# Seven block products in place of eight for some pairs of up products, and four down groups in place of three

## The chip, the cores and the metric

The kernel runs on one core of a Trainium2 chip. The metric is the device time of one execution in microseconds. The kernel before takes 1869.24 us (median of 3 runs, 1866.7 to 1871.07).

## The reference, cut to what matters

One step of a small diffusion backbone with 640 tokens (128 context tokens and 512 latent tokens), width 1024 and two layers: the first mixes tokens with a gated DeltaNet, the second with neighbourhood attention. Each layer ends with a gated feed-forward part, and that is what the change touches:

```python
def conv_ffn(h, w_up, conv_w, conv_b, w_down):
    u = dwconv_centred(h @ w_up, conv_w) + conv_b
    val, gate = jnp.split(u, 2, axis=-1)
    return (jax.nn.silu(gate) * val) @ w_down
...
xs = xs + g2s * conv_ffn(rmsnorm(xs, norm2_g[l]) * (1.0 + sc2s) + sh2s, ffn_w_up[l], ...)
```

The up projection is 1024 x 5632, the down projection 2816 x 1024, all in float32. The shifts, scales and gates of a layer come from a product of 1024 x 6144 with the conditioning vector.

## The kernel before, in words

Activations lie transposed: partitions carry channels, the free axis carries the 640 tokens. A float32 factor is split into a high part, rounded to the fast matmul format fp32r (`hh`, `wh`, by ScalarE), and the remainder (`hl`, `wl`, by VectorE). A product of a 128-channel tile with a k-tile is three matmuls, high x high, high x low, low x high (`pass3`, L388 to L390), accumulated in PSUM over eight k-tiles. The tokens are cut at 384, so that a product has matmuls of 384 and of 256 columns.

A feed-forward layer (`ffn`) goes through 22 pairs of up products. A pair is a value tile (`uv`) and its gate tile (`ug`): `weights` loads 512 KB on SP's queue into one of two staging tiles (`wst`), casts and subtracts it into one of two weight buffers (`wh`, `wl`), and the product goes into a PSUM tile of two banks, of which there are two (tag `d`). `conv` (L440, L445) takes it out: one ScalarE activation for the middle tap, four VectorE steps for the outer taps of the two token groups. Then silu, the product of value and gate, and the split into `F` follow. After 8, 7 and 7 pairs the down products of that group of `F` tiles run for the eight output tiles (`rdn`), and `residual` (L454) adds them, times the gate of the modulation, into the residual stream `X` with three VectorE steps an output tile. The last group is cut into two halves of tokens (`into_residual_split`), so that the next norm begins while the second half is still multiplied.

Modulation vectors that are needed later are computed beside this by VectorE alone (`ada_rows`, L252): a row tile of 256 KB is loaded and two multiply-reduce instructions of 512 columns follow. `between` hands out those of 32 modulation tiles after the products of the first layer, and `Na.run` those of 16 more in the attention stage; eight are left to the second layer. In the feed-forward layers their loads are issued from GpSimd's queue, in the attention stage from SP's.

The order of instructions on each engine is fixed when the kernel is built: a scheduler takes for each engine the earliest instruction of the program whose inputs it expects to be ready, so work without dependencies is drawn forward into gaps. `issue_after` (through `behind`, `chained`) ties one instruction's place behind another's; `high_priority` moves a block forward. At run time every engine and queue works strictly in that order.

Of the kernel before, what the change touches and what calls it, by code (L numbers as in the profile page):

```python
# [57 lines left out]
GROUPS = ((0, 8), (8, 15), (15, 22))  # L58
# [29 lines left out]
class Net:  # L88
    def __init__(self, ctx, tc, a):
# [5 lines left out]
        self.wide = False  # L95
        self.hooks, self.strict = [], False
# [313 lines left out]
    def dense(self, src, name, base=UBASE, halves=HALVES_U):  # L410
        w = self.weights(src, KT, name)
        ps = self.pd.tile([128, 1024], F32, tag="d", name=f"d{name}")
        for cols in halves:
            self.prod(ps, base, w, KT, self.hmov, cols)
        return ps
# [4 lines left out]
    def dense_many(self, srcs, names, norm):  # L420
# [11 lines left out]
        return [ps for _, ps in out]  # L432

# [24 lines left out]

    def into_residual(self, srcs, kt, movs, l, gi, name, first={}, between=None):
        late = []  # L460
        for m in range(KT):
            w = first.get(m) or self.weights(srcs[m], kt, f"{name}{m}")
            ps = self.pd.tile([128, 1024], F32, tag="d", name=f"r{name}{m}")
            if m < 2:
                late.append((w, ps))
                for half in (0, 1):
                    self.prod(ps, RBASE, w, kt, movs, HALVES_R[half], ks=range(kt - 1))
                if m < 1:
                    continue
            else:  # L470
                late = [(w, ps)]
            for i, (w, ps) in enumerate(late, m + 1 - len(late)):
                for half in (0, 1):
                    self.prod(ps, RBASE, w, kt, movs, HALVES_R[half], ks=range(kt - 1, kt) if m < 2 else None)
                for half in (0, 1):
                    self.residual(ps, i, half, l, gi)
            if between and m > 1:
                between(None)

    def half_bank(self, name, i, half):  # L480
        if self.wide and i % 2 == 1:
            return self.pa.tile([128, 512], F32, tag="g", name=name)
        return self.pd.tile([128, 1024 if self.wide else 512], F32, tag="d", name=name)
# [41 lines left out]
    def ffn(self, l, fp, norm, norms, between=None):  # L525
# [3 lines left out]
        fcb = self.smv("fcb").rearrange("p (l t) -> p l t", l=2)[:, l]  # L529
        def hold(name, n):  # L530
            if name[-1] == "5":
                return fp.tile([128, 2 * W], F32R, tag="F", name=name, bufs=9)[:, 16 : 16 + n]
            size = KT if name[-1] in "01" else NFT - GROUPS[-1][0]
            return fp.tile([128, size * 128], F32R, tag=name[:2] + name[-1], name=name, bufs=1)[:, :n]

        for grp, (g0, g1) in enumerate(GROUPS):
            fs = []
            srcs = [a["w_dn"][l, m][:, g0 * 128 : g1 * 128] for m in range(KT)]
            first = {}
            for i in range(g0, g1):  # L540
                if i >= g1 - 2:
                    m = i - g1 + 2
                    first[m] = self.weights(srcs[m], g1 - g0, f"dn{l}{grp}{m}", None, hold)
                up, names = [a["w_up"][l, i], a["w_up"][l, NFT + i]], [f"uv{l}{i}", f"ug{l}{i}"]
                if i == 0:
                    with self.behind(self.marks):
                        pv, pg = self.dense_many(up, names, norm)
                else:
                    pv = self.dense(up[0], names[0])
                    if between:  # L550
                        between(None)
                    pg = self.dense(up[1], names[1])
                with self.tc.high_priority(FHP if i == g1 - 1 else 0):
                    yv = fp.tile([128, W], F32, tag="yv", name=f"yv{l}{i}", bufs=2)
                    yg = fp.tile([128, W], F32, tag="yg", name=f"yg{l}{i}", bufs=2)
                    self.conv(yv, pv, fcw[:, i], fcb[:, i : i + 1])
                    self.conv(yg, pg, fcw[:, NFT + i], fcb[:, NFT + i : NFT + i + 1])
                    c = slice(0, W)
                    nc.scalar.activation(yg[:, c], yg[:, c], AF.Silu)
                    nc.vector.tensor_tensor(yv[:, c], yv[:, c], yg[:, c], ALU.mult)  # L560
                    f = fp.tile([128, 2 * W], F32R, tag="F", name=f"F{l}{i}", bufs=9).rearrange("p (a w) -> p a w", a=2)
                    nc.scalar.copy(f[:, 0, c], yv[:, c])
                    nc.vector.tensor_tensor(f[:, 1, c], yv[:, c], f[:, 0, c].bitcast(F32), ALU.subtract)
                fs.append(f)
                if between:
                    between(i)
            movs = lambda k, fs=fs: (fs[k][:, 0, :], fs[k][:, 1, :])
            if g1 < NFT:
                self.into_residual(srcs, g1 - g0, movs, l, 5, f"dn{l}{grp}", first, between)
            else:  # L570
# [1094 lines left out]
```

## Time and profile before

| | us |
|---|---|
| median of 3 runs | 1869.24 |
| profiled execution | 1872.86 |
| its span, first to last instruction | 1871.1 |
| TensorE busy, of the span | 1790.4 (96%) |
| VectorE busy | 1257.4 (67%) |
| ScalarE busy | 725.9 (39%) |
| GpSimd busy | 290.3 (16%) |

The first feed-forward layer runs from about 583 to 1050 us, the attention stage to about 1350, the second feed-forward layer from about 1397 to the end. The mean granted TensorE clock is 0.98. Matmuls are pipelined: their listed durations overlap, and the ends of VectorE's instructions overlap a little with the next start. A row of a group of instructions gives engine, operation, output and inputs by the program's names, shape, count, then busy time in us and mean duration in ns, then the idle time before them and what ended it. L12 is line 12 of the kernel.

### The profile page before, as it was taken

The numbers are of one execution on the slowest core, as the hardware profiler recorded it, in microseconds if no ns is written. First come the engines' busy times: TensorE is split into PE (matmuls) and PEld (weight loads), VectorE is DVE, ScalarE is ACT, GpSimd is POOL, SyncE is SP. The second block draws the span as 40 slices with busy tenths as digits, with TensorE's granted clock in tenths as the row PEclk, the third lists the DMA queues.
The fourth block names the chain that finished last, engine by engine and source line by source line (L and its number), as shares of the span: only waits on it lengthen the run. The fifth ranks groups of instructions, "written<-read, shape, count | busy, mean of one in ns | idle before, by whom it ended". The sixth has DMA issues, their size and how long they took to land.

```text
span 1871.1 us, 34463 instructions
## 1 busy us (share of the span) xinstructions
PE 1790.4 (96%) x13587; PEld 1702.7 (91%) x13587; DVE 1257.4 (67%) x3093; ACT 725.9 (39%) x1461; POOL 290.3 (16%) x498
## 2 busy tenths in 40 slices
PE   6889999799999999999999999999999999999998
PEld 5878988598899999999999988888899999999998
DVE  6797867487678999754465799555689643543664
ACT  4553445264444341241243444444454322332343
POOL 0245103417003112100000212111141000000000
PEclk9898999799999999999999999999999999999999
DMA  7133233232242455441222344222334312222231
GB/s 299 61 85 108 54 124 108 76 96 61 64 158 86 155 182 163 132 163 54 87 90 80 124 152 139 75 78 65 96 107 136 102 48 78 88 62 77 89 92 57
DMA packets 102482, 194.17 MB, mean 104 GB/s; under 512 B 39496, under 2 KB 59034, under 8 KB 99560
## 3 DMA queue, kind: packets, MB, share of 16 engines
q1 hardware_dynamic: 93376, 161.57, 27.5%
q0 software_dynamic: 8400, 29.87, 5.2%
q8 instruction: 107, 1.75, 0.4%
q14 instruction: 55, 0.45, 0.1%
q10 hardware_dynamic: 544, 0.52, 0.1%
HBM read 183.09 MB, written 12.46 MB: 105 GB/s over the span
## 4 chain that ended last, share of the span: by engine, by line
PE 50%; DVE 4%; issue 2%; DMA 1%; ACT 1%; POOL 0%; DVEq 0%; POOLq 0%; ACTq 0%
PE duv L388 4%; PE duv L390 4%; PE duv L389 4%; PE dug L388 4%; PE dug L389 4%; PE dug L390 4%; PE rdn L388 4%; PE rdn L389 4%; PE rdn L390 4%; PE dqn L388 1%; PE dvn L388 1%; PE no L1346 1%; PE s L1289 1%; PE dvn L390 1%; PE dvn L389 1%
## 5 line engine op out<-in xcount | busy, mean ns | idle before, releaser
L388 PE MATMUL duv<-hh,whuv 128*128 128x256 f32 (+1 forms) x704 | 217.2, 309 | 5.9 <-DVE yv L445 4.0
L388 PE MATMUL rdn<-F,whdn 128*128 128x384 f32 (+1 forms) x704 | 216.1, 307 | 3.3 <-DVE X L454 3.3
L390 PE MATMUL duv<-hh,wluv 128*128 128x256 f32 (+1 forms) x704 | 216.7, 308 | 0.3 <-DVE wluv L378 0.3
L389 PE MATMUL duv<-hl,whuv 128*128 128x256 f32 (+1 forms) x704 | 216.5, 308 | 0.0
L389 PE MATMUL dug<-hl,whug 128*128 128x256 f32 (+1 forms) x704 | 215.9, 307 | 0.0
L390 PE MATMUL dug<-hh,wlug 128*128 128x256 f32 (+1 forms) x704 | 215.9, 307 | 0.0
L388 PE MATMUL dug<-hh,whug 128*128 128x256 f32 (+1 forms) x704 | 215.9, 307 | 0.0
L389 PE MATMUL rdn<-F,whdn 128*128 128x384 f32 (+1 forms) x704 | 215.5, 306 | 0.0
L390 PE MATMUL rdn<-F,wldn 128*128 128x384 f32 (+1 forms) x704 | 215.5, 306 | 0.0
L388 PEld LDWEIGHTS duv<-hh,whuv 128*128 128x128 f32 x704 | 132.8, 189 | 6.4 <-ACT yg L440 4.6
L388 PEld LDWEIGHTS rdn<-F,whdn 128*128 128x128 f32 x704 | 132.4, 188 | 4.0 <-issue 2.1
L454 DVE SCALAR_TENSOR_TENSOR X<-rdn,mods,X 128x128 f32<-128x128 f32 (+1 forms) x144 | 54.9, 434 | 117.6 <-PE rdn L390 117.4
L390 PEld LDWEIGHTS duv<-hh,wluv 128*128 128x128 f32 x704 | 132.9, 189 | 0.6 <-DVE wluv L378 0.6
L389 PEld LDWEIGHTS duv<-hl,whuv 128*128 128x128 f32 x704 | 132.7, 189 | 0.0
L388 PEld LDWEIGHTS dug<-hh,whug 128*128 128x128 f32 x704 | 132.4, 188 | 0.0
L390 PEld LDWEIGHTS dug<-hh,wlug 128*128 128x128 f32 x704 | 132.3, 188 | 0.0
L389 PEld LDWEIGHTS rdn<-F,whdn 128*128 128x128 f32 x704 | 132.2, 188 | 0.0
L390 PEld LDWEIGHTS rdn<-F,wldn 128*128 128x128 f32 x704 | 132.2, 188 | 0.0
L389 PEld LDWEIGHTS dug<-hl,whug 128*128 128x128 f32 x704 | 132.1, 188 | 0.0
L376 ACT CAST whdn<-wstdn 128x896 fp32r<-128x896 f32 (+1 forms) x48 | 47.0, 979 | 209.1 <-PE rdn L389 120.9
L376 ACT CAST whug<-wstug 128x1024 fp32r<-128x1024 f32 x44 | 46.2, 1050 | 142.9 <-PE dug L389 119.4
L378 DVE TENSOR_TENSOR wldn<-wstdn,whdn 128x896 fp32r<-128x896 f32 (+1 forms) x48 | 54.4, 1133 | 56.7 <-ACT whdn L376 56.7
(710 smaller groups left out, 4803.3 us busy)
## 6 DMA issues: line engine op xcount, KB each, us to landing
wstuv<-w_up SPq DMA_DIRECT2D x44, 512.0 KB, 3.5
wstug<-w_up SPq DMA_DIRECT2D x44, 512.0 KB, 3.6
adat<-w_ada SPq DMA_DIRECT2D x20, 1024.0 KB, 5.0
adr<-w_adar POOLq DMA_DIRECT2D x80, 256.0 KB, 3.2
wstdn<-w_dn SPq DMA_DIRECT2D x32, 448.0 KB, 3.4
wstdn<-w_dn SPq DMA_DIRECT2D x16, 512.0 KB, 3.6
adr<-w_adar SPq DMA_DIRECT2D x32, 256.0 KB, 2.9
wstqT<-w_gin SPq DMA_DIRECT2D x8, 512.0 KB, 4.4
```

The lines of the kernel that those rows point to most:

```text
L376: nc.scalar.copy(wh[:, c], st[:, c])
L378: ins = eng.tensor_tensor(wl[:, c], st[:, c], wh[:, c].bitcast(F32), ALU.subtract).ins
L388: nc.tensor.matmul(out, a, mh, start=first, stop=False)
L389: nc.tensor.matmul(out, a, ml, start=False, stop=False)
L390: ins = nc.tensor.matmul(out, b, mh, start=False, stop=last).ins
L454: nc.vector.scalar_tensor_tensor(x, ps[:, base + c0 : base + c1], self.mod(l, gi, m, v), x, ALU.mult, ALU.add)
L1289: nc.tensor.matmul(ss[e][:, o], qb[H[e]], kk[H[e]], start=True, stop=True, tile_position=(64 * e, 0))
L1346: nc.tensor.matmul(O[H[e], cb * 128 : cb * 128 + 128], v_, p_, start=(j == 0), stop=(j == 2), tile_position=(0, 64 * e),)
```

## The change

Four pairs of the first layer (11, 14, 17, 20) and seven of the second (8, 10, 12, 14, 16, 18, 20) are multiplied by blocks (`pair`). The pair's weights are a 2 x 2 block matrix (value and gate; first and last four k-tiles: v0, v1, g0, g1), the activations another (first and last four k-tiles; tokens 0 to 319 and 320 to 639). Seven products of sums of blocks, in Winograd's arrangement, give the four output blocks that eight give otherwise. Each product has 4 k-tiles, 3 passes and 320 columns. The sums of weight blocks are made by GpSimd, each of the seven weight blocks is split into high and low by `quarter` (two blocks share a weight buffer), the products are added up into SBUF tiles by ScalarE copies (2), VectorE (5) and GpSimd (2), and the convolution reads those tiles. The four sums of activation blocks and their splits are made once a layer by `blocks`, in steps after pairs 6 to 10 and 3 to 7 (`TSTEP`).

The other pairs (`dense_pair`) write half tiles, one PSUM bank each, of five banks (a new pool `pf` of the layer); `conv_parts` works half by half, with six VectorE steps and two activations in place of four and one. The down groups are four (6, 5, 5, 6 inputs), each after the first pair of the next group (`downs`), with half banks taken in turn from two tags (`half_bank`: three banks `g`, five banks `d`). There are seven `F` tiles in place of nine, and the last group's weights lie in the tiles of the activation blocks. Eight modulation tiles, those of the gate of the second layer's attention, move from the first feed-forward layer to the attention stage, which calls its sums after each of six steps a head pair in place of four; the numbers of calls in the layers are listed in `SUMS`. The second layer's matmuls are now chained in program order as the first layer's were. The attention's PSUM pool `pd` is opened behind the first layer, its output tile `O` moves into it, and the scratch for GpSimd's DMAs is set to 8192 bytes.

```diff
-GROUPS = ((0, 8), (8, 15), (15, 22))
+GROUPS = ((0, 6), (6, 11), (11, 16), (16, 22))
+NH = W // 2
+BYBLOCK = ((11, 14, 17, 20), (8, 10, 12, 14, 16, 18, 20))
+TSTEP = ((6, 7, 7, 8, 8, 9, 9, 10), (3, 4, 4, 5, 5, 6, 6, 7))
+SUMS = ((0, 3, 3, 3, 3, 3, 1, 1, 1, 1, 1, 2, 3, 3, 2, 3, 3, 2, 3, 3, 2, 0), (0, 3, 3, 3, 3, 2, 2))
...
+    def dense_pair(self, srcs, names, banks, norm=None):
+
+        ws, pss = [], []
+        for src, name, b in zip(srcs, names, banks):
+            ws.append(self.weights(src, KT, name, self.nc.gpsimd if norm else None))
+            pss.append(self.halves_of(b, f"d{name}"))
+        if norm:
+            self.hooks, self.strict = [(HK2[0], norm), (HK2[1], norm)], False
+        order = [(i, j) for i in range(2) for j in range(2)] if norm else [(i, j) for j in range(2) for i in range(2)]
+        for i, j in order:
+            self.prod(pss[j][i], -HALVES_U[i][0], ws[j], KT, self.hmov, HALVES_U[i])
+        return [[(*cols, t) for cols, t in zip(HALVES_U, ps)] for ps in pss]
...
+    def conv_parts(self, y, parts, wv, bias):
+
+        nc = self.nc
+        for lo, hi, t in parts:
+            nc.scalar.activation(y[:, lo:hi], t[:, : hi - lo], AF.Identity, scale=wv[:, 1:2], bias=bias)
+        for lo, hi, t in parts:
+            for tap, sh in ((0, -1), (2, 1)):
+                for s0, s1 in ((PC, PC + 128), (SC, SC + 512)):
+                    a, b = max(s0, s0 - sh, lo - sh), min(s1, s1 - sh, hi - sh)
+                    if a < b:
+                        nc.vector.scalar_tensor_tensor(
+                            y[:, a:b], t[:, a + sh - lo : b + sh - lo], wv[:, tap : tap + 1], y[:, a:b],
+                            ALU.mult, ALU.add,
...
+    def quarter(self, src, name, lo=None):
+
+        nc, n = self.nc, src.shape[1]
+        if self.spare is None:
+            self.spare = [
+                self.wp.tile([128, KT * 128], F32R, tag=t, name=f"{t}{name}", bufs=2) for t in ("wh", "wl")
+            ]
+            wh, wl = (t[:, :n] for t in self.spare)
+        else:
+            wh, wl = (t[:, 512 : 512 + n] for t in self.spare)
+            self.spare = None
+        nc.scalar.copy(wh, src)
+        (lo or nc.vector).tensor_tensor(wl, src, wh.bitcast(F32), ALU.subtract)
+        return wh, wl
...
+    def blocks(self, fp, l):
+        nc, TT = self.nc, self.nc.vector.tensor_tensor
+        for k in range(4):
+            b = [fp.tile([128, W], F32, tag=f"c{n}", name=f"b{n}{l}{k}", bufs=1) for n in "vg"]
+            for i in range(2):
+                TT(b[i], self.hh[:, k + 4 * i].bitcast(F32), self.hl[:, k + 4 * i].bitcast(F32), ALU.add)
+            b11, b12, b21, b22 = b[0][:, :NH], b[0][:, NH:], b[1][:, :NH], b[1][:, NH:]
+            TT(b11, b12, b11, ALU.subtract)
+            yield
+            TT(b12, b22, b12, ALU.subtract)
+            TT(b22, b22, b11, ALU.subtract)
+            TT(b21, b21, b22, ALU.subtract)
+            for t, x in zip(self.T, (b11, b22, b12, b21)):
+                nc.scalar.copy(t[:, k, 0], x)
+                TT(t[:, k, 1], x, t[:, k, 0].bitcast(F32), ALU.subtract)
+            yield
...
+    def pair(self, l, i, fp, pf):
+
+        nc, a = self.nc, self.a
+        P, V = nc.gpsimd.tensor_tensor, nc.vector.tensor_tensor
+        g = fp.tile([128, KT * 128], F32, tag="wsg", name=f"wsg{l}{i}", bufs=1)
+        nc.sync.dma_start(g, a["w_up"][l, NFT + i])
+        v = self.wp.tile([128, KT * 128], F32, tag="wst", name=f"wsv{l}{i}", bufs=WSTB)
+        self.load = nc.sync.dma_start(v, a["w_up"][l, i]).ins
+        v0, v1, g0, g1 = v[:, :512], v[:, 512:], g[:, :512], g[:, 512:]
+        s1, s2 = (fp.tile([128, 512], F32, tag=t, name=f"{t}{l}{i}", bufs=1) for t in ("s1", "s2"))
+        first, last = (lambda k: (self.hh[:, k], self.hl[:, k])), (lambda k: (self.hh[:, k + 4], self.hl[:, k + 4]))
+        L, R = (0, NH), (NH, W)
+        p1, p5 = (fp.tile([128, NH], F32, tag=f"p{n}", name=f"p{n}{l}{i}", bufs=1) for n in "15")
+        cv, cg = (fp.tile([128, W], F32, tag=f"c{n}", name=f"c{n}{l}{i}", bufs=1) for n in "vg")
+        cv0, cv1, cg0, cg1 = cv[:, :NH], cv[:, NH:], cg[:, :NH], cg[:, NH:]
+
+        def product(n, src, movs, cols):
+            w = self.quarter(src, f"p{n}{l}{i}")
+            ps = pf.tile([128, 512], F32, tag="d", name=f"pp{l}{i}{n}", bufs=5)
+            for k in range(4):
+                self.pass3(ps[:, :NH], w, k, movs(k), cols, k == 0, k == 3)
+            return ps[:, :NH]
+
+        P(s1, g0, g1, ALU.add)
+        x = product(5, s1, self.tmov(0), L)
+        nc.scalar.copy(p5, x)
+        P(s2, s1, v0, ALU.subtract)
+        P(g0, v0, g0, ALU.subtract)
+        x = product(1, v0, first, L)
+        nc.scalar.copy(p1, x)
+        P(s1, v1, s2, ALU.subtract)
+        x = product(6, s2, self.tmov(1), L)
+        V(cg1, x, p1, ALU.add)
+        P(cv1, cg1, p5, ALU.add)
+        x = product(3, s1, last, R)
+        V(cv1, x, cv1, ALU.add)
+        x = product(2, v1, last, L)
+        V(cv0, x, p1, ALU.add)
+        x = product(7, g0, self.tmov(2), L)
+        V(cg0, x, cg1, ALU.add)
+        P(cg1, cg0, p5, ALU.add)
+        x = product(4, g1, self.tmov(3), L)
+        V(cg0, x, cg0, ALU.add)
+        self.spare = None
+        return [(0, W, cv)], [(0, W, cg)]
...
+    def downs(self, l, grp, fs):
+
+        g0, g1 = GROUPS[grp]
+        n = g1 - g0
+        for m in range(KT):
+            w = self.weights(self.a["w_dn"][l, m][:, g0 * 128 : g1 * 128], n, f"dn{l}{grp}{m}")
+            for half, c in enumerate(HALVES_R):
+                ps = self.half_bank(f"rdn{l}{grp}{m}{half}", 0, half)
+                self.prod(ps, -c[0], w, n, lambda k: (fs[g0 + k][:, 0], fs[g0 + k][:, 1]), c)
+                with self.tc.high_priority(HP):
+                    self.residual(ps, m, half, l, 5, -c[0])
...
+        g, d = (self.pa, "g", 3), (pf, "d", 5)
+        direct = ((d, d), (d, d))
+        self.banks = [g, d]
...
+            names = [f"uv{l}{i}", f"ug{l}{i}"]
+            grp = after.get(i)
+            if i not in BYBLOCK[l]:
+                up = [a["w_up"][l, i], a["w_up"][l, NFT + i]]
+                with self.behind(self.marks if i == 0 else ()):
+                    pv, pg = self.dense_pair(up, names, direct, norm if i == 0 else None)
             else:
-                return self.into_residual_split(
-                    srcs, g1 - g0, movs, l, 5, f"dn{l}{grp}", norms, hold, (6, 7), first=first
-                )
+                pv, pg = self.pair(l, i, fp, pf)
...
+                f = fp.tile([128, 2 * W], F32R, tag="F", name=f"F{l}{i}", bufs=7).rearrange("p (a w) -> p a w", a=2)
+                nc.scalar.copy(f[:, 0], yv)
+                nc.vector.tensor_tensor(f[:, 1], yv, f[:, 0].bitcast(F32), ALU.subtract)
+            fs[i] = f
+            for _ in range(TSTEP[l].count(i)):
+                next(steps, None)
+            if between:
+                between(i)
+            if grp is not None:
+                self.downs(l, grp, fs)
...
-        sums = net.ada_rows([(1, m, t) for m in (3, 4) for t in range(KT)], self.ap_, 2, self.nc.sync)
+        sums = net.ada_rows([(1, m, t) for m in (2, 3, 4) for t in range(KT)], self.ap_, 2, self.nc.sync)
...
-                if i > 1:
-                    next(sums, None)
+                next(sums, None)
...
-        sums = net.ada_rows([(0, 5, t) for t in range(KT)] + [(1, m, t) for m in (0, 1, 2) for t in range(KT)], fp, ADB, nc.gpsimd)
+        sums = net.ada_rows([(0, 5, t) for t in range(KT)] + [(1, m, t) for m in (0, 1) for t in range(KT)], fp, ADB, nc.gpsimd)
...
-    nc = bacc.Bacc("TRN2", target_bir_lowering=False, num_devices=1)
+    nc = bacc.Bacc("TRN2", target_bir_lowering=False, num_devices=1, dynamic_dma_scratch_size=8192)
```

## Rows read from the trace of the kernel before

**Rows 1.** Busy time by stretch: length, PE, PEld, DVE, ACT, POOL, clock, DMA.
```profile
583.00:1030.00 447.00, 440.24 (x3034) 438.93 (x3034) 316.28 (x636) 141.28 (x171) 43.75 (x75) 1.00 0.39 121
...
1420.00:1840.00 420.00, 419.08 (x2851) 418.75 (x2850) 226.62 (x384) 135.87 (x162) 4.30 (x8) 1.00 0.26 81
```

**Rows 2.** TensorE in order of time: start, duration, line, operation.
```profile
649.70 0.34 PE L390 MATMUL dug<-hh,wlug 128*128 128x384 f32 x1
...
653.00 0.28 PE L388 MATMUL dug<-hh,whug 128*128 128x256 f32 x1
...
655.72 0.33 PE L388 MATMUL duv<-hh,whuv 128*128 128x384 f32 x1
...
1504.15 0.34 PE L388 MATMUL dug<-hh,whug 128*128 128x384 f32 x1
...
1511.22 0.34 PE L388 MATMUL rdn<-F,whdn 128*128 128x384 f32 x1
```

**Rows 3.** The same view: matmuls behind a wait, in brackets length and releaser.
```profile
600.61 0.41 PE L388 MATMUL duv<-hh,whuv 128*128 128x384 f32 x1 [1.66 <-DVE yv L445]
...
712.84 0.41 PE L388 MATMUL rdn<-F,whdn 128*128 128x384 f32 x1 [1.92 <-DVE X L454]
...
771.05 0.41 PE L388 MATMUL duv<-hh,whuv 128*128 128x384 f32 x1 [2.37 <-DVE yv L445]
...
866.35 0.41 PE L388 MATMUL rdn<-F,whdn 128*128 128x384 f32 x1 [0.46 <-DVE X L454]
...
1410.69 0.41 PE L388 MATMUL duv<-hh,whuv 128*128 128x384 f32 x1 [1.88 <-ACT yg L440]
```

**Rows 4.** Busy time by stretch, just behind the wait at 1410.
```profile
1411.20:1414.60 3.40, 3.40 (x13) 3.40 (x12) 3.37 (x7) 1.94 (x2) 0.00 (x0) 0.50 0.26 105
```

**Rows 5.** Busy time by stretch: pairs with sums (first) and without.
```profile
656.20:711.00 54.80, 54.72 (x383) 54.52 (x381) 53.99 (x118) 20.10 (x24) 9.83 (x18) 1.00 0.58 180
780.00:835.00 55.00, 55.00 (x386) 55.00 (x385) 32.83 (x51) 21.86 (x26) 5.57 (x7) 1.00 0.51 161
1459.00:1514.00 55.00, 55.00 (x377) 55.00 (x376) 31.94 (x48) 22.64 (x26) 0.00 (x0) 1.00 0.30 94
```

**Rows 6.** Groups of VectorE and ScalarE: count, busy us, mean ns.
```profile
L445 DVE SCALAR_TENSOR_TENSOR yg<-dug,sm,yg 128x511 f32<-128x511 f32 x88 | 65.1, 740 | 0.0
L445 DVE SCALAR_TENSOR_TENSOR yg<-dug,sm,yg 128x127 f32<-128x127 f32 x88 | 30.1, 342 | 1.8 <-ACT yg L440 1.7
L378 DVE TENSOR_TENSOR wlug<-wstug,whug 128x1024 fp32r<-128x1024 f32 x42 | 51.3, 1222 | 58.1 <-ACT whug L376 57.9
L376 ACT CAST whug<-wstug 128x1024 fp32r<-128x1024 f32 x44 | 46.2, 1050 | 142.9 <-PE dug L389 119.4 <-PE rdn L389 21.7 <-issue 1.4
```

**Rows 7.** GpSimd and VectorE in order of time, as in Rows 2.
```profile
800.96 1.92 DVE L445 SCALAR_TENSOR_TENSOR yg<-dug,sm,yg 128x127 f32<-128x127 f32 x4
...
1035.23 0.74 DVE L348 SCALAR_TENSOR_TENSOR hl<-nt,mods,hh 128x256 fp32r<-128x256 f32 x2
1035.89 1.12 DVE L343 SCALAR_TENSOR_TENSOR nt<-X,scg,nrs 128x256 f32<-128x256 f32 x3
1036.25 2.41 POOL L378 TENSOR_TENSOR wlkn<-wstkn,whkn 128x1024 fp32r<-128x1024 f32 x1 [1.59 <-ACT whkn L376]
1036.94 2.00 DVE L348 SCALAR_TENSOR_TENSOR hl<-nt,mods,hh 128x256 fp32r<-128x256 f32 x1
...
1355.99 1.29 POOL L378 TENSOR_TENSOR wlno<-stg,whno 128x512 fp32r<-128x512 f32 x1 [1.78 <-ACT whno L376]
...
1357.30 0.69 DVE L378 TENSOR_TENSOR wlno<-wstno,whno 128x512 fp32r<-128x512 f32 x1 [2.54 <-ACT whno L376]
```

**Rows 8.** Busy time by stretch, one head pair of the attention each.
```profile
1073.80:1110.10 36.30, 35.43 (x270) 30.62 (x269) 33.72 (x99) 16.79 (x40) 5.98 (x12) 1.00 0.49 152
...
1146.40:1181.30 34.90, 33.95 (x268) 29.88 (x267) 24.76 (x74) 15.61 (x38) 5.95 (x12) 1.00 0.31 98
1181.30:1215.90 34.60, 33.77 (x270) 29.80 (x269) 18.67 (x55) 15.40 (x39) 5.67 (x12) 1.00 0.26 76
```

More of the change, by code (lines that the diff above doesn't have):

```diff
@@ L95, in __init__ @@
         self.wide = False
+        self.banks, self.turn, self.spare = None, 0, None
         self.hooks, self.strict = [], False
@@ L408, in hmov, with halves_of @@
         return self.hh[:, k, :], self.hl[:, k, :]
[L410 to L415, printed above, removed]
+    def halves_of(self, banks, name):
+        return [pool.tile([128, 512], F32, tag=tag, name=f"{name}{i}", bufs=bufs) for i, (pool, tag, bufs) in enumerate(banks)]
     def keep(self, pool):
@@ L456, in residual @@
                 )
[L459 to L478, printed above, removed]
     def half_bank(self, name, i, half):
+        if self.banks:
+            self.turn += 1
+            pool, tag, bufs = self.banks[self.turn % len(self.banks)]
+            return pool.tile([128, 512], F32, tag=tag, name=name, bufs=bufs)
         if self.wide and i % 2 == 1:
@@ L529, in ffn @@
         fcb = self.smv("fcb").rearrange("p (l t) -> p l t", l=2)[:, l]
+        last = len(GROUPS) - 1
         def hold(name, n):
[L531 to L569, printed above, removed]
-            else:
-                return self.into_residual_split(
-                    srcs, g1 - g0, movs, l, 5, f"dn{l}{grp}", norms, hold, (6, 7), first=first
-                )
@@ L576 @@
+        self.spare = None
+        g0, g1 = GROUPS[last]
+        srcs = [a["w_dn"][l, m][:, g0 * 128 : g1 * 128] for m in range(KT)]
+        movs = lambda k: (fs[g0 + k][:, 0, :], fs[g0 + k][:, 1, :])
+        norm = self.into_residual_split(srcs, g1 - g0, movs, l, 5, f"dn{l}{last}", norms, hold, (6, 7))
+        self.banks = None
+        return norm
 SCHED = (
@@ L1311, in attend @@
         nc.vector.tensor_copy(pt, t[:, :384])
-        O = net.pa.tile([128, 512], F32, tag="o", name=f"no{p}", bufs=1)
+        O = net.pd.tile([128, 512], F32, tag="o", name=f"no{p}", bufs=1)
         for cb in range(4):
@@ L1548, in build @@
         net.chain = True
-        norm = net.ffn(0, fp, norm, normer(1, 1), between)
+        norm = net.ffn(0, fp, pf, norm, normer(1, 1), between)
         net.chain = False
-    with tc.tile_pool(name="nao", bufs=1, reuse_waits="tile") as nao:
+    with tc.tile_pool(name="pd", bufs=2, space=PSUM, reuse_waits="tile") as net.pd, tc.tile_pool(name="nao", bufs=1, reuse_waits="tile") as nao:
         net.align(nao, SHIFT)
@@ L1563, in build @@
             )
-    with tc.tile_pool(name="fp1", bufs=2, reuse_waits="tile") as fp:
+    with tc.tile_pool(name="fp1", bufs=2, reuse_waits="tile") as fp, ps_ffn(1) as pf:
         sums = net.ada_rows([(1, 5, t) for t in range(KT)], fp, ADB, nc.gpsimd)
         next(sums)
-        turns = chain([0] * 4, [2] * 8)
         def between(i):
-            for _ in range(next(turns, 0)):
+            for _ in range(SUMS[1][i] if i < len(SUMS[1]) else 0):
                 next(sums, None)
-        run(net.ffn(1, fp, norm, lambda half, order: final_half(net, np_, half, order), between))
+        net.chain = True
+        run(net.ffn(1, fp, pf, norm, lambda half, order: final_half(net, np_, half, order), between))
 def pack(inputs):
```

35 lines of the change are left out of this document (26 added, 9 removed).

## The prediction

> **What bounds the kernel now.** I read the stages first: busy time of each engine and granted clock by stretch. In both feed-forward layers TensorE is busy for nearly the whole stretch (440 of 447 us, 419 of 420) and VectorE for 71% and 54% [rows 1]. So a layer lasts as long as its matmuls, plus the few places where TensorE waits, and only fewer matmul columns or fewer waits shorten it. The listed duration of a matmul (0.34 us with 384 columns) is not its price: matmuls overlap. The price is the distance from one start to the next. In the first layer 19 matmuls of 384 columns take 653.00 - 649.70 = 3.30 us, 0.1737 us each, and 24 of 256 columns take 655.72 - 653.00 = 2.72 us, 0.1133 us each. In the second layer one up product, 24 matmuls of each shape, takes 1511.22 - 1504.15 = 7.07 us, 0.1473 us a matmul against 0.1435 [rows 2]: a quick and a slow pace, both at a granted clock of 1.00 [rows 5], for which no row gives a cause. A pair of up products (48 matmuls of each shape) costs 13.78 us at the quick and 14.14 us at the slow pace.
>
> Then the waits of TensorE, by name [rows 3]. Each layer stalls once behind its first pair (1.66 and 1.88 us): the next product needs a PSUM tile that the convolution of the first has not released. After the second of these the granted clock is 0.50 (the 1.2 GHz level) for 3.4 us, 13 matmuls instead of some 23, so 1.7 us more [rows 4]. Down groups stall on their residual adds (1.92, and three times 0.46), and one pair waited 2.37 us for a convolution queued behind other VectorE work.
>
> Last, how much room VectorE has. While modulation sums are there to fill its gaps it is 99% busy (53.99 of 54.80 us), and once they are done 60% and 58% [rows 5]. It fills itself with whatever is ready, so its 99% is not its need.
>
> **The columns.** A block pair has 7 products of 4 k-tiles and 3 passes on 320 columns: 84 matmuls. No row has 320 columns; halfway between the two shapes is 0.1435 us (quick) or 0.1473 (slow), so 12.05 or 12.37 us. That saves 1.73 or 1.77 us a pair. Bounds: at the pace of the 256 shape it would be 9.5 us (4.3 saved), at that of the 384 shape 14.6 (0.8 lost); I take the middle, since both neighbours lie close to one line through the column count. Four pairs in the first layer and seven in the second: 4 x 1.73 + 7 x 1.75 = 19.2 us less.
>
> **Stalls that go.** Half tiles in five banks: pair 1 begins in the fifth bank, and its second half comes 24 x 0.1737 = 4.2 us later, longer than both start stalls. The down groups get eight half banks in turn and begin one pair after their last input is made. I take away 1.66 + 1.88 + 1.7 (the clock stretch) + 1.92 + 3 x 0.46 = 8.5 us. The 2.37 us I leave: its cause, a VectorE that fills itself with sums, remains. What is late next at the starts is the weights of pair 1, which have had one product's time.
>
> **VectorE, GpSimd and ScalarE.** From [rows 6, 7], with 0.08 us off each duration for the overlap (four convolution steps run as 1.92 us where their means, 0.740 and 0.342 twice each, add up to 2.16): a direct pair needs 7.5 us now, and 8.0 with its convolution in six pieces instead of four (256 columns by the line through 127 and 511: 0.476). A block pair needs seven subtractions of 512 columns (0.69 each), five adds of 320 (0.49 by the line through 512 and 1024), the convolution from SBUF as now, product and split of 640 (0.82 each by that line): 4.3 + 2.05 + 3.7 + 1.5 = 11.5 us, against 12.05 us of TensorE. The prepared block operands add 4 x 4.8 = 19 us a layer, 16 more rounds of residual adds some 9 us. In the second layer, from pair 8, a block and a direct pair together need 19.5 of 25.8 us. In the first, 16 parts of sums leave (24 us). All this hides under TensorE as long as VectorE is under 100%; uncovered, all of it would be some 100 us. ScalarE needs about 8 us a block pair and is not near a limit.
>
> GpSimd gets six two-input adds a block pair. From 1.29 us for 512 columns and 2.41 for 1024 [rows 7]: 4 x 1.29 + 2 x 0.87 = 6.9 us, which fits. But a VectorE subtraction of 256 columns from two SBUF tiles, which runs at 0.37, took 2.00 us, from 1036.94 to 1038.94, while GpSimd's ran until 1038.66 [rows 7]. Three steps with one PSUM input, begun at 1035.89 and overlapping the same GpSimd operation, took their usual 0.37 each. So each GpSimd add can hold up VectorE's weight subtractions and the convolutions from SBUF, not its reads of PSUM. Counted in full, two pairs need 19.5 + 6.9 = 26.4 of 25.8 us; counted at half, 23. The Trainium skill (SBUF — State Buffer, "SBUF: two separate sides") says that a VectorE instruction with two SBUF inputs and a GpSimd one that reads SBUF lock each other out for a whole instruction; the 2.00 us agree. By that rule in full, the sum would be that of the third rival below.
>
> **New waits.** Quarters share two weight buffers. The next pair's first weights go into the buffer of products 2 and 7, free at 6 x 1.72 = 10.3 us of 12.05. In 1.7 us the cast (1.05 [rows 6]) and the subtraction (1.22) must run; the third matmul of the next pair needs the latter 0.35 us after the end, so 0.3 us is late with both engines idle. VectorE is not idle: its own convolution (1.9 us) and the last adds are queued about there, and behind the waiting subtraction queue the convolution and the PSUM releases. 0.3 to 2.5 us a pair; I take 1.2, a convolution half in the way: 11 x 1.2 = 13 us. The 0.3 is the floor by construction. GpSimd's queue also carries the loads of modulation rows in the first layer, each of which waits for its buffer; an add behind it waits too. This lies inside the 1.2.
>
> **The attention stage.** It gets 32 of the modulation reductions more (24 us of VectorE) and 16 loads on SP's queue. The three head pairs that carry the present 64 take 36.3 us (two of them) and 34.9 against 34.6 without [rows 8]: 3.7 us for 64, so 1.9, say 2, for 32 (0 to 4).
>
> **Pace.** About 245 us of the second layer (1411 to 1515 and 1526 to 1670, read as in [rows 2]; a stretch of it is in [rows 5], 377 matmuls in 55 us against 386) run at the slow pace: 245 x (1 - 13.78/14.1) = 5.4 us. The changed kernel may run all at the quick one (5 less) or the first layer too at the slow one (447 x 0.026 = 12 more). Nothing says which; I take 0.
>
> **Sum.** -19.2 - 8.5 + 13 + 2 = -12.7 us. The profiled execution took 1872.9 us (span 1871.1, 1.8 around it), 3.6 over the median of the runs, 1869.2. The same difference on the median gives 1856.5; I say 1857.
>
> **Rivals.**
> (1) Nearly no waits: 0.3 us a block pair, quick pace, nothing in attention: -19.2 - 8.5 + 3.3 - 5.3 = -29.7, so 1840. For it: VectorE's 58% now. Against: the 0.3 us supposes engines that stand ready.
> (2) The waits eat the gain: 2.3 us a block pair, (19.2 + 8.5 - 2) / 11. About 1869.
> (3) Slower: GpSimd's adds shut VectorE out of its weight subtractions, as at 1036.94. Within a block pair VectorE then needs 11.5 + 6.9 = 18.4 us against 12.05; if the direct pair beside it makes up only half of the 6.4 us, TensorE waits 3.2 us a block pair, 35 us in all in place of 13: 1857 + 22 = 1879 (with nothing made up, 1914). It decides from 2.3 us a pair. For it: the 2.00 us; against: the 5.8 us of room in each direct pair, and three of the six adds need nothing of the pair's products and can run before it.
> (4) The columns are not cheaper: 320 cost what 384 cost, 14.6 us a pair, 28 us more than in the sum: 1885. Against: 384 to 256 columns is nearly in proportion.
>
> **Chances.** Forecast 0.50 (its own range 1848 to 1864), (1) 0.18, (2) 0.11, (3) 0.16, (4) 0.05. About 0.2%, 3.7 us, is what a measurement of this kernel can tell from no change. Faster: 0.50 + 0.18 = 0.68; same: 0.11; slower: 0.16 + 0.05 = 0.21. The range 1840 to 1880 leaves out half of (1), half of (3) and most of (4), about 0.2.
>
> **What would show it.** Starts of 320-column matmuls 0.140 to 0.148 us apart (0.17 is rival 4). No TensorE wait behind pair 0 of a layer, none on the residual. A wait at the first weights after each block pair, on the weight subtraction or cast, about 1 us; over 2.3 us is rival 3, and there VectorE subtractions of 512 columns would last well over 0.69 us beside GpSimd adds. Attention stage 2 us longer. The prediction is wrong if the layers lose less than 8 us between them, or if TensorE's waits sit inside block pairs, on VectorE's adds into the block sums, rather than behind them.

## The result and the profile after

The changed kernel takes 1880.2 us (median of 20 runs) against 1868.6 for the kernel before (20 runs): ratio 1.0059, 95% interval 1.0043 to 1.0076. I had forecast 1857, faster; it is slower.

The lengths of the stages come from the profiled execution of each kernel: from the start of the first matmul of a stage to that of the next (first `duv` of a layer, first `dqn` of the attention, last matmul). The medians are of all timed runs; the experiments' names are explained below. A reduction is counted from here on as one row tile, which is two VectorE instructions; the forecast counted instructions.

```
kernel                                layer 1  attention  layer 2   median   ratio to before
before                                  465.2      344.9    471.2   1868.6
after                                   482.7      351.0    457.9   1880.2   1.0059 [1.0043, 1.0076]
e1  no block pairs                      457.3      355.3    460.8   1861.1   0.9947 [0.9925, 0.9968]
e2  block pairs in layer 2 only         462.8      352.7    458.0   1854.9   0.9931 [0.9912, 0.9949]
e3  table loads early                   490.7      347.9    459.8   1883.4   1.0076 [1.0055, 1.0096]
e4  two adds on VectorE                 478.7      348.1    459.1   1878.7   1.0057 [1.0035, 1.0078]
e5  32 reductions left out, layer 1     470.5      349.6    459.4   1867.1   0.9997 [0.9984, 1.0010]
e6  next weights ahead                  470.2      350.1    457.6   1870.8   1.0015 [1.0000, 1.0030]
e7  as e2, reductions doubled           457.3      351.6    497.6   1891.3   1.0128 [1.0109, 1.0148]
e8  as e2, sums back in layer 1         458.9      348.8    458.9   1854.9   0.9935 [0.9915, 0.9955]
e9  e3 + e5 + e6 together               460.3      350.4    459.8   1852.9   0.9918 [0.9903, 0.9932]
e10 e6 + table loads in pairs 3 to 10   473.1      350.6    457.2   1865.0   0.9983 [0.9969, 0.9998]
```

Each row of stages is one execution. The instructions ahead of the first layer, the same and in the same order on every engine before and after, took 583.3 us in the one profile and 575.4 in the other; the identical first layers of e1, e2 and e7 took 457.3, 462.8 and 457.3. So a few us between two stages are scatter, and the profiled executions (1872.9 and 1875.4) lie closer together than the medians.

The two layers, which got the same kind of change, went opposite ways: the second is 13.3 us shorter, the first 17.5 longer. Busy time by stretch of the changed kernel (layer 1, attention, layer 2), against [rows 1]:

```profile
575.40:1058.20 482.80, 462.43 (x3147) 457.81 (x3146) 370.69 (x788) 179.31 (x277) 70.75 (x87) 0.99 0.34 104
1058.20:1409.10 350.90, 337.04 (x2546) 301.37 (x2545) 270.82 (x764) 158.78 (x377) 66.95 (x108) 0.99 0.39 119
1409.10:1867.00 457.90, 451.74 (x3121) 448.30 (x3120) 341.84 (x665) 190.90 (x299) 69.37 (x60) 1.00 0.27 83
```

VectorE is busy for 77% of the first layer and 75% of the second, GpSimd for 15% in both. By these averages the layers are alike, and neither engine is the bound. TensorE's idle time by releaser tells them apart. First layer (575 to 1058), then the second (1409 to 1867); the columns are the sum in us, the number of waits, the longest:

```profile
PE duv L395 <- DVE wluv L383: 6.8, 3, 3.6
PE pp L393 <- ACT whp L551: 3.3, 2, 2.2
PE dug L393 <- DVE cv L611: 2.5, 1, 2.5
PE dug L393 <- DVE cg L618: 2.1, 1, 2.1
PE rdn L395 <- DVE wldn L383: 1.6, 2, 1.4
PE pp L395 <- DVE wlp L552: 1.4, 3, 0.9
PE duv L393 <- DVE yv L459: 1.3, 1, 1.3
...
PE duv L395 <- DVE wluv L383: 3.7, 7, 0.8
```

In the second layer seven small waits at the weight subtraction `wluv`, six of them behind block pairs, are all that matters up to the closing norm. In the first there are 15 waits of 20.3 us in all (two short groups are left out above), none of them before pair 11.

The columns themselves: 24 matmuls of 320 columns, first and last.

```profile
769.83 0.30 PE L393 MATMUL pp<-T,whp 128*128 128x320 f32 x1
...
773.19 0.31 PE L395 MATMUL pp<-hh,wlp 128*128 128x320 f32 x1
```

3.36 us over 23 distances is 0.146 us each, so 84 take 12.3 us and a pair saves 1.5.

Now one wait of the first layer, behind pair 17. In order of time:

```profile
948.38 1.05 ACT L381 CAST whuv<-wstuv 128x1024 fp32r<-128x1024 f32 x1 [0.21 <-PE pp L394]
...
949.13 0.48 DVE L615 TENSOR_TENSOR cg<-pp,cg 128x320 f32<-128x320 f32 x1
...
950.20 1.46 POOL L599 TENSOR_TENSOR s<-wsg 128x512 f32<-128x512 f32 x1 [5.29 <-DMA wsg<-w_up]
951.62 0.86 POOL L616 TENSOR_TENSOR cg<-cg,p 128x320 f32<-128x320 f32 x1
952.51 0.49 DVE L618 TENSOR_TENSOR cg<-pp,cg 128x320 f32<-128x320 f32 x1 [1.98 <-POOL cg L616]
952.92 1.22 DVE L383 TENSOR_TENSOR wluv<-wstuv,whuv 128x1024 fp32r<-128x1024 f32 x1
...
954.19 0.69 PE L395 MATMUL duv<-hh,wluv 128*128 128x384 f32 x1 [3.64 <-DVE wluv L383]
```

Read it backwards. TensorE waits 3.64 us for `wluv`, whose cast had ended at 949.4; it is queued behind the last block sum (L618), and that waits 1.98 us for GpSimd's add (L616), which stands behind the next block pair's first weight sum (L599), which waited for its load. The same place in the second layer, behind pair 12:

```profile
1602.39 0.49 DVE L615 TENSOR_TENSOR cg<-pp,cg 128x320 f32<-128x320 f32 x1
1602.79 1.22 DVE L383 TENSOR_TENSOR wluv<-wstuv,whuv 128x1024 fp32r<-128x1024 f32 x1
...
1604.06 0.45 PE L395 MATMUL duv<-hh,wluv 128*128 128x384 f32 x1 [0.59 <-DVE wluv L383]
...
1604.77 0.49 DVE L618 TENSOR_TENSOR cg<-pp,cg 128x320 f32<-128x320 f32 x1 [0.76 <-POOL cg L616]
```

Here `wluv` stands ahead of L618, and TensorE waits 0.59. Which stands first was settled when the kernel was built. What follows the long wait costs once more: the granted clock of the 6.8 us behind it is 0.58, for the most part at the lower level (0.50, 1.2 GHz).

```profile
954.20:961.00 6.80, 6.80 (x25) 6.80 (x26) 4.47 (x7) 1.54 (x3) 0.00 (x0) 0.58 0.45 154
```

The two other such stretches of the layer have 0.63 (from 853.2) and 0.59 (from 1000.2) for 3.4 us each. With (1 - clock) times length the three lose 5.5 us.

And a wait of another sort, behind pair 14. The bias table's third load goes out at 858.6, its fourth at 864.1, the weights of pair 16 at 865.3:

```profile
876.07 1.05 ACT L381 CAST whuv<-wstuv 128x1024 fp32r<-128x1024 f32 x1 [10.74 <-DMA wstuv<-w_up]
877.14 1.23 DVE L383 TENSOR_TENSOR wluv<-wstuv,whuv 128x1024 fp32r<-128x1024 f32 x1 [10.56 <-ACT whuv L381]
878.29 0.48 DVE L611 TENSOR_TENSOR cv<-pp,cv 128x320 f32<-128x320 f32 x1
...
878.83 0.39 PE L393 MATMUL dug<-hh,whug 128*128 128x256 f32 x1 [2.54 <-DVE cv L611]
```

DMA issues of 862 to 882 (KB, us from issue to landing):

```profile
cols<-bt POOLq DMA_DIRECT2D x1, 752.0 KB, 11.0
wstuv<-w_up SPq DMA_DIRECT2D x1, 512.0 KB, 10.7
wstug<-w_up SPq DMA_DIRECT2D x1, 512.0 KB, 11.2
```

The median of `wstuv` over the whole kernel is 3.5 us. VectorE stood 10.56 us at a subtraction whose weights were late; behind it in its queue was L611, which reads a product's PSUM bank, and TensorE needed that bank.

### The profile page after: what moved, and what is told of

Same layout as the page of the kernel before. It is cut to its first block, busy times and chain, and to the rows that moved or that the text cites. A ratio compares the mean times of both kernels' runs of the same rounds, so it can differ in the third digit from the quotient of the medians.

```text
span 1873.6 us, 34951 instructions
## 1 busy us (share of the span) xinstructions
PE 1775.3 (95%) x13455; PEld 1683.2 (90%) x13455; DVE 1403.4 (75%) x3479; ACT 791.3 (42%) x1652; POOL 371.8 (20%) x548
## 4 chain that ended last, share of the span: by engine, by line
PE 56%; DVE 17%; issue 10%; DMA 6%; POOL 5%; ACT 3%; SPq 1%; POOLq 0%; DVEq 0%; ACTq 0%
PE rdn L395 4%; PE rdn L393 4%; PE rdn L394 4%; PE duv L395 3%; PE duv L393 3%; PE duv L394 3%; PE dug L393 2%; PE dug L394 2%; PE dug L395 2%; POOL lY L947 2%; POOL lP L941 2%; DVE yv L459 1%; DVE yg L459 1%; DVE adj L257 1%; DVE adr L257 1%
## 5 line engine op out<-in xcount | busy, mean ns | idle before, releaser
L395 PE MATMUL duv<-hh,wluv 128*128 128x256 f32 (+1 forms) x528 | 164.5, 312 | 10.4 <-DVE wluv L383 10.4
L395 PE MATMUL rdn<-F,wldn 128*128 128x256 f32 (+1 forms) x560 | 171.7, 307 | 2.2 <-DVE wldn L383 2.1
L393 PE MATMUL rdn<-F,whdn 128*128 128x256 f32 (+1 forms) x560 | 171.5, 306 | 0.7 <-ACT whdn L381 0.7
L394 PE MATMUL rdn<-F,whdn 128*128 128x256 f32 (+1 forms) x560 | 171.3, 306 | 0.0
L393 PE MATMUL dug<-hh,whug 128*128 128x256 f32 (+1 forms) x528 | 161.8, 306 | 5.2 <-DVE cv L611 2.5
L393 PE MATMUL duv<-hh,whuv 128*128 128x256 f32 (+1 forms) x528 | 163.9, 310 | 1.3 <-DVE yv L459 1.3
L394 PE MATMUL dug<-hl,whug 128*128 128x256 f32 (+1 forms) x528 | 161.5, 306 | 0.0
L395 PE MATMUL dug<-hh,wlug 128*128 128x256 f32 (+1 forms) x528 | 161.5, 306 | 0.0
L484 DVE SCALAR_TENSOR_TENSOR X<-rdn,mods,X 128x256 f32<-128x256 f32 (+1 forms) x192 | 77.7, 435 | 74.6 <-PE rdn L395 74.2
L393 PEld LDWEIGHTS rdn<-F,whdn 128*128 128x128 f32 x560 | 105.1, 188 | 0.9 <-ACT whdn L381 0.9
L394 PEld LDWEIGHTS rdn<-F,whdn 128*128 128x128 f32 x560 | 105.1, 188 | 0.1
L459 DVE SCALAR_TENSOR_TENSOR yv<-duv,sm,yv 128x127 f32<-128x127 f32 (+1 forms) x198 | 77.4, 432 | 13.1 <-ACT yv L453 12.6
L459 DVE SCALAR_TENSOR_TENSOR yg<-dug,sm,yg 128x127 f32<-128x127 f32 (+1 forms) x198 | 77.3, 432 | 8.6 <-ACT yg L453 8.1
```

The source lines that it names most:

```text
L393: nc.tensor.matmul(out, a, mh, start=first, stop=False)
L394: nc.tensor.matmul(out, a, ml, start=False, stop=False)
L395: ins = nc.tensor.matmul(out, b, mh, start=False, stop=last).ins
L459: nc.vector.scalar_tensor_tensor(y[:, a:b], t[:, a + sh - lo : b + sh - lo], wv[:, tap : tap + 1], y[:, a:b], ALU.mult, ALU.add,)
L484: nc.vector.scalar_tensor_tensor(x, ps[:, base + c0 : base + c1], self.mod(l, gi, m, v), x, ALU.mult, ALU.add)
```

## The experiments

Theories at the start: **A**, the first layer's loss comes from weight loads late beside the table loads and from queue orders; **B**, GpSimd's adds lock VectorE out (the third rival); **C**, the restructuring (half banks, four groups) is itself the loss.

**e1, e2.** `BYBLOCK = ((), ())` and `BYBLOCK = ((), (8, ..., 20))`, with `TSTEP` to match.

> All up products direct in both layers (no product by blocks, no block operands made); the four groups, the half banks and the moved modulation sums stay as in the changed kernel. Stage lengths of before: first layer 465.2, attention 344.9, second layer 471.2; of the changed kernel 482.7, 351.0, 457.9. Theory A (the four block pairs of the first layer lose time to late weight loads beside the table loads and to queue orders; the rest does what was forecast): first layer 460 to 465, attention 349 to 351, second layer 466 to 469, total about 1867, ratio to before 0.999. Rival C (the restructuring itself is the loss: half banks, a down group more): first layer still 478 or more, total 1885 to 1895, ratio 1.010 or more. Rival B (GpSimd's adds of the block pairs hold VectorE up) expects the same as A here.

> Products by blocks in the seven pairs of the second layer only; the first layer all direct. Theory A: first layer 460 to 465, attention 349 to 351, second layer 457 to 459 as in the changed kernel; total about 1858, ratio 0.994. Rival C: first layer 478 or more, total 1877 or more, ratio above 1.003. Rival B: second layer's seven pairs pay the lock too, so its gain is the pace and the start alone and e1's second layer is as short as this one's, within 3 us.

C falls: without block pairs the new structure is faster than before. The four block pairs of the first layer cost 482.7 - 457.3 = 25.4 us in the profiles (19.9 against e2's slower run of the same first layer) and 1880.2 - 1854.9 = 25.3 in the medians. The seven of the second gain 2.8 in the profiles, little more than the scatter of that layer (457.9 to 459.8 in the five kernels that have it as in the changed one), and the medians (6.2 apart) have overlapping intervals, so this gain is not shown by itself. From start to start of the matmuls these 2.8 are 10.3 saved by columns less 4.8 at the seven `wluv`, 0.9 at down weights and some 2 spread thinly. B is not decided by e2: it asked for an e1 whose second layer is within 3 us of e2's, and 2.8 is. e1's second layer is 5 us below the least that A said: the slow pace of before is gone.

**e3, e4.** e3: `if 1 <= i <= 7:` with two steps of the table loads a pair, in place of `if i >= TAB:`.

```
-        P(cv1, cg1, p5, ALU.add)      e4, and the same for P(cg1, cg0, p5, ...)
+        V(cv1, cg1, p5, ALU.add)
```

> The loads of the bias table and masks of the attention stage are issued during pairs 1 to 7 of the first layer, two steps a pair, in place of later ones beside the block pairs; the rest as in the changed kernel. Theory A: the weight loads beside block pairs 11, 14 and 17 take 3 to 4 us in place of 10 to 11, and the waits behind them go: first layer 474 to 477 in place of 482.7, total about 1873, ratio 1.002. If the late loads are hidden anyway or the table loads only shift the same wait to pairs 1 to 7: first layer 481 to 485, ratio 1.006. Rival B: first layer unchanged within 2 us.

> Two of the six GpSimd additions of a block pair (the two sums of 320 columns that take in product 5) run on VectorE instead; the four sums of weights stay on GpSimd. Theory A: the 3.6 us wait behind the pair at 954 us goes, and some entry waits shrink by the 0.5 us that an add takes less: first layer 477 to 480, second layer 457 to 459, total about 1877, ratio 1.004. Rival B (VectorE locked out by GpSimd): a third of the lost time goes in both layers: first layer 474 or less and second layer 455 or less, ratio 1.000 or less. If VectorE's load is what counts: slower, first layer 485 or more.

e3 misses, and so does what A said of e4's wait. In e3 the waits of `dug` (2.5 and 2.1) are gone as A said, but the reductions came later and now lay beside the block pairs (56 of their 96 VectorE instructions run behind the first block matmul, against 8 in the changed kernel); three waits at `wluv` add up to 9.6 us. Yet all waits together are no longer than before (19.3 us for 20.3): the 8.0 us that the layer is longer are, about half each, stretches at half clock and the slow pace, which the last section finds in unchanged code too. e4's profiled run is its quickest (1871.2; median 1878.7); its stages lie about where A put them, and the ratio is that of the changed kernel, so B's third of the loss did not come back. Its row behind pair 17 corrected A: no block sum runs on GpSimd any more, and the wait is still 2.99.

```profile
951.25 1.56 POOL L599 TENSOR_TENSOR s<-wsg 128x512 f32<-128x512 f32 x1 [10.25 <-DMA wsg<-w_up]
...
951.58 1.77 DVE L459 SCALAR_TENSOR_TENSOR yv<-cv,sm,yv 128x511 f32<-128x511 f32 x1
953.27 0.48 DVE L618 TENSOR_TENSOR cg<-pp,cg 128x320 f32<-128x320 f32 x1
953.67 1.21 DVE L383 TENSOR_TENSOR wluv<-wstuv,whuv 128x1024 fp32r<-128x1024 f32 x1
...
954.94 0.44 PE L395 MATMUL duv<-hh,wluv 128*128 128x384 f32 x1 [2.99 <-DVE wluv L383]
```

It is the place in VectorE's queue, whatever holds the queue up. Here 1.0 us of it is B's: the convolution step of 511 columns took 1.77 us in place of 0.74 [rows 6] beside GpSimd's next weight sum (L599). So A was split: **S** (the reductions beside the block pairs), **T** (the table loads), **Q** (the queue orders).

**e5 to e8.** e5: `ada_rows` for the 16 parts of `(0, 5)` alone. e6:

```
+            with self.tc.high_priority(ahead):      # 40 behind a block pair, else 0
+                ws.append(self.weights(...))
...
+            with self.tc.high_priority(60):
+                w = self.quarter(src, f"p{n}{l}{i}")
```

e7: `(5, 0, 1)` for `(5,)` in the second layer's `ada_rows`, with the first layer's `SUMS`. e8: the tiles of modulation 2 back in the first layer.

> As the changed kernel, but 32 of the 48 modulation reductions of the first layer are left out, those that follow the first 16 (the shift and scale of the next norm are set to zero); so from pair 6 on no reduction and no load of their rows stands beside the block pairs, while the table loads do. First layer 482.7 in the changed kernel, 457.3 without block pairs. If the reductions and their loads are the cause (theory S): first layer 458 to 465. If the table loads are (theory T): 472 to 480, the waits for weights at 865 and 878 still there. If queue orders of the block pairs by themselves are (theory Q): 474 to 480, the waits behind pairs 17 and 20 (3.8 and 2.7 us) still there.

> As the changed kernel, but the next pair's first weight subtraction stands ahead of the last sum of the block pair on VectorE's queue behind pairs 17 and 20 of the first layer (in the second layer it stands there already); some casts of quarters move a place or two. Theory Q: the waits of 3.8 and 2.7 us behind these pairs shrink to under 1 us each, and the half-clock stretches behind them go: first layer 474 to 477, total about 1873. Theories S and T: those waits move elsewhere (the weights are late by themselves): first layer 480 to 484, total 1878 to 1882.

> Products by blocks in the second layer only, and that layer is given the first layer's modulation work: the 32 reductions of the shift and scale are computed a second time there, with the first layer's timetable (26 of 46 steps beside the block pairs), loads on GpSimd's queue. Second layer 458.0 without them, first layer 457 to 463. Theory S: second layer 475 or more. Theories T and Q: 458 to 463, since VectorE has room beside the seven block pairs (19.5 us of work in 25.8).

> Products by blocks in the second layer only, and the 16 reductions that the change moved into the attention stage computed in the first layer again, three steps a pair. Attention 352.7 with the change's place, 344.9 before. If the moved reductions cost the attention stage 4 us and the first layer has room for them: attention 347 to 349, first layer 457 to 463, second 458, total about 1851, ratio 0.991. If the first layer, without room, pays for them: first layer 466 or more, total 1856 to 1862.

e7 makes the second layer ill in the same way: 39.6 us longer, of which 20.1 are seven waits at `wluv`, with stretches of about half the clock behind them. The row of a wait, what is ahead of it, and the stretch after:

```profile
1587.91 3.58 DVE L459 SCALAR_TENSOR_TENSOR yv<-cv,sm,yv 128x127 f32<-128x127 f32 x4
1588.14 0.87 POOL L616 TENSOR_TENSOR cg<-cg,p 128x320 f32<-128x320 f32 x1 [0.77 <-DVE cg L615]
...
1589.42 1.25 POOL L599 TENSOR_TENSOR s<-wsg 128x512 f32<-128x512 f32 x1 [0.42 <-DMA wsg<-w_up]
1591.41 0.48 DVE L618 TENSOR_TENSOR cg<-pp,cg 128x320 f32<-128x320 f32 x1
1591.81 1.21 DVE L383 TENSOR_TENSOR wluv<-wstuv,whuv 128x1024 fp32r<-128x1024 f32 x1
...
1593.08 0.69 PE L395 MATMUL duv<-hh,wluv 128*128 128x384 f32 x1 [3.59 <-DVE wluv L383]
```
```profile
1593.10:1598.60 5.50, 5.50 (x18) 5.50 (x19) 4.99 (x10) 0.74 (x1) 0.55 (x1) 0.52 0.48 133
```

What the reductions do is not mainly to take time. In VectorE's queue as built, `wluv` stands ahead of L618 in e2 at six of the second layer's seven block pairs (behind the other comes a down group), and right behind L618 in e7 at the same six. The scheduler takes the earliest instruction of the program that it expects to be ready; my reading, from these orders alone, is that a VectorE filled with reductions comes free so late in the plan that L618 counts as ready by then. The runs do not show this. In the changed kernel the last of the reductions starts at 940.9, ahead of the waits at 954 and 1000; in e7 it starts at 1602.8, and waits of 2.6 to 3.6 us go on at 1661, 1693, 1790 and 1822. So the order is turned even at pairs that have no reduction beside them, and how stays open.

e6 changes only the order (the next pair's weights and the quarters move forward), all reductions in place, and gets from the first layer what e5 gets by leaving them out: 470.2 and 470.5, 12.5 and 12.2 less; in the medians 9.4 and 13.1 less. The waits at `pp`, where the quarters count, hardly change (4.4 us for 4.7). Behind pair 17:

```profile
952.52 1.22 DVE L383 TENSOR_TENSOR wluv<-wstuv,whuv 128x1024 fp32r<-128x1024 f32 x1
...
953.79 0.44 PE L395 MATMUL duv<-hh,wluv 128*128 128x384 f32 x1 [0.25 <-DVE wluv L383]
...
955.74 0.49 DVE L620 TENSOR_TENSOR cg<-pp,cg 128x320 f32<-128x320 f32 x1 [2.00 <-POOL cg L618]
```

The last sum (L620 here) still waits 2.00 us for GpSimd; TensorE no longer does. None of the three half-clock stretches between 850 and 1004 is left; the first, behind a `pp` wait that is still there, may have gone by chance. So Q is shown, S works through Q at pairs 17 and 20 (in e5 `wluv` stands ahead of L618 there), and e5's expectation for S (458 to 465) missed because of T: the waits of pairs 14 to 16 stand in e5 and e6 alike.

e8: attention 3.9 us shorter than e2, which is within the scatter (see below), and no gain in the median (1851 was expected). e2 and e8 are the fastest kernels here that leave nothing out, 0.7% below before.

**e9, e10.**

> Three things at once in the first layer: the 32 reductions of the next norm's shift and scale left out (set to zero), the next pair's weight subtraction ahead of the last block sum on VectorE, the table loads issued in pairs 1 to 7. If the first layer's extra cost over the second is these three and no more (two block sums queued wrongly, reductions beside the blocks, table loads beside the weight loads): the waits of 2.35, 2.86, 1.47, 2.26 and 1.51 us between 850 and 910 go, first layer 457 to 461 with its four block pairs, against 457.3 with none; total about 1856, ratio 0.994. If something else in the first layer's block pairs is dear: first layer 465 or more.

> As e6 (the next pair's weight subtraction ahead of the last block sum), and the table loads issued in pairs 3 to 10, two steps a pair; all reductions in place. If the late weight loads of e6 (11.7 us of waits between 857 and 910) are due to the table loads beside them, and pairs 3 to 10 have room: first layer 460 to 463, total about 1860, ratio 0.996. If the reductions, held up behind the table loads in the same queue, come to lie beside the block pairs instead: new waits at pairs 11 to 15 of 5 to 10 us, first layer 466 to 472, total 1866 to 1872.

e9 fits: 460.3, and its waits in the first layer are

```profile
PE pp L393 <- ACT whp L552: 2.2, 1, 2.2
PE duv L395 <- DVE wluv L383: 1.2, 3, 0.5
PE pp L395 <- DVE wlp L553: 0.4, 1, 0.4
```

So order, reductions and table loads hold all but 3 us of the 25. e10 keeps the reductions and misses its first expectation: of the waits of 857 to 910 1.6 us are left, which shows T, but the first layer is 473.1, a little over what the second foretold; 3 to 4 us of that are the slow pace. Behind the four table loads in GpSimd's queue stand pair 11's weight sums, which wait for their load, and only then the next reductions' loads; VectorE is full of reductions behind pair 11, and the down weights come late:

```profile
701.38 2.40 POOL L219 DMA_DIRECT2D cols<-bt  x4
760.56 1.29 POOL L604 TENSOR_TENSOR s<-s,wsv 128x512 f32<-128x512 f32 x1 [56.78 <-DMA wsv<-w_up]
...
771.76 1.17 POOL L239 DMA_DIRECT2D adr<-w_adar  x2
```
```profile
795.69 0.69 PE L395 MATMUL rdn<-F,wldn 128*128 128x384 f32 x1 [4.82 <-DVE wldn L383]
```

A place where the table loads harm nothing was not found.

## Why the prediction was wrong, by its own steps

**The step that failed** is "New waits": "0.3 to 2.5 us a pair; I take 1.2", with the sentence that GpSimd's loads lie "inside the 1.2", and the sentence under VectorE that all the added work "hides under TensorE as long as VectorE is under 100%". For the second layer the step holds: seven waits, 0.2 to 0.8 us, 3.7 in all where 8.4 were put down. In the first layer, the four pairs bring 25.4 us where the sum had -1.73 + 1.2 each, -2.1: 20.3 us of waits stand in the place of 4.8, and 5.5 us of lower clock behind them. VectorE stood at 77%, and what was late was late by its place in a queue. I had named what queues behind the waiting subtraction, but not what the plan would put ahead of it when more reductions share the layer, and I had assumed one order for both layers. The table loads were in none of my terms, though they lie in the same stretch before and after.

**Columns.** 0.146 us, close to the forecast's slow figure (0.1473) though at the quick pace of its neighbours: 1.5 us a pair, some 16 in all for 19.2.

**Stalls.** No wait behind pair 0 in either layer, none on the residual: right. e1 measures them with the pace: first layer 7.9 less (1.66 + 1.92 + 0.46 were forecast for it, 4.04, and the 2.37 that I left went too, 6.41). Second layer 10.4 less: 1.88 + 1.7 + 0.92 forecast, 4.5, and the pace that I had put at nothing (5.4; its own figures, 248 us at 13.78 against 14.1, give 5.6). That the pace turned quick is not shown to be the change's doing: the same instructions ran at either pace (last section).

**Attention.** +2 (0 to 4) forecast; 6.1 measured, 3.0 to 10.4 over the kernels of the table but e8. e8, without the moved reductions, has 348.8, still 3.9 more than before, and lies inside the range of the ten kernels with them (347.9 to 355.3, mean 350.7). So their cost is not shown, though 350.7 - 348.8 = 1.9 is about the forecast, and the sum had no term for the rest (`nps` waits 1.9 at the start, stretches at half clock), which was not followed up.

**The sum.** -12.7 forecast, about +11.7 measured. e2 keeps everything but the first layer's block pairs and has -13.7; the forecast without its four pairs' -2.1 would be -10.6. That these are close is in part luck: the attention cost more than the sum had, and the pace gave what it had not.

**The rivals.** The time came out at the third one's 1879, but not by its mechanism: e4 took a third of GpSimd's adds away (a quarter of their time by the forecast's figures) and nothing came back, and the second layer, with seven block pairs and the same adds, gains. Nor does the lock tell the layers apart: VectorE instructions that overlap a GpSimd one and last over a quarter longer than the median of their kind without one lose 10.4 us in the first layer of the changed kernel and 16.2 in the second. It is seen all the same: in e7 four convolution steps from SBUF lasted 3.58 us beside L616 and L599, against 1.92 alone [rows 7]. By the rule cited in the forecast (the Trainium skill, SBUF — State Buffer, "SBUF: two separate sides") both sit on one lock; the 3.58 agree. In these rows it costs TensorE something where a weight subtraction stands behind it. The fourth (320 columns as dear as 384) falls with 0.146. The first sign of being wrong came: the layers were to get at least 8 us shorter between them, and in the profiles they grew by 17.5 - 13.3 = 4.2. The other was put as waits inside the block pairs: they are there (`pp`, 4.7 us), on weight quarters rather than on the block sums, but the larger part is behind the pairs, where I had looked for 1 us.

## What to carry to other kernels

An engine at 77% can still stop the one that bounds the kernel: ask, for each instruction that the bound engine waits for, what stands ahead of it in its queue, and whether other work in the same stretch changes that order. The same edit in two stages can have two prices; find what one stage has beside it that the other has not (here reductions and table loads) before one price is put on both. To test an order, move only the order: e6 got 12.5 of the 25 us back in the profile, 9.4 in the medians, without taking any work away.

## What the runs showed of the hardware that was not expected

A weight load of 512 KB on SP's queue took 10.7 to 11.2 us beside a 752 KB table load of GpSimd's queue, against a median of 3.5.

The two paces of TensorE are not a matter of the code. e1 and e2 have the same first layer, instruction by instruction on every engine; from 600 to 640 us, at a granted clock of 1.00 and busy throughout, one did 282 matmuls and the other 272:

```profile
600.00:640.00 40.00, 40.00 (x282) 40.00 (x281) 39.50 (x95) 16.57 (x23) 6.03 (x11) 1.00 0.46 152
```
```profile
600.00:640.00 40.00, 40.00 (x272) 40.00 (x272) 38.59 (x91) 16.30 (x23) 6.36 (x12) 1.00 0.44 144
```

Over the whole layer the mean distance is 0.1136 us (256 columns) and 0.1733 (384) in e1, 0.1156 and 0.1748 in e2; with some 1580 of each that makes the 5.5 us between their first layers. What sets the pace stays open.

A wait's length alone doesn't tell whether the clock falls behind it: behind 2.70 us in e6 (at 882) 3.4 us were at 1.00, behind 2.56 in the changed kernel (at 1000) at 0.59. The `pp` wait of pair 14 is nearly the same in both, 2.18 us in the changed kernel and 2.19 in e6: the granted clock behind it is 0.63 in the one and 1.00 in the other.
